# Issuing the on-chip hops of split queries and keys from ScalarE instead of SyncE

## Chip, core and metric

One core of a Trainium2 chip runs the whole kernel as one program. The metric is the device time in microseconds of that core, the median of three runs. Five engines work side by side, each through its own instructions in order: TensorE (PE), VectorE (DVE), ScalarE (ACT), GpSimd (POOL) and SyncE (SP), which issues the DMA transfers. An instruction waits for semaphores that other engines or finished transfers raise.

## What is computed

Two blocks of a network act on 512 tokens of width 1024. The first is a layer of dilated attention, gated linear attention and block attention followed by an MLP with a squared relu; the second has two layers, each with a Fourier mix, attention with rotary tables over the tokens and a context of 256 tokens, a two-way recurrent scan, and a gated MLP. The context goes through the first of the two layers as well. Cut to its frame:

```python
def reference(x, ..., final_norm_w, c_2, ctx_2, ...):
    x = first_block(x, norm1_w, w_in, ..., final_norm_w)
    return second_block(x, c_2, ctx_2, c_ctx_2, w_ada_2, ...)

def hybrid_layer(x, ...):                 # first block
    proj = rmsnorm(x, norm1_w) @ w_in
    y_a, y_b, y_c = dilated_attention(...), gla(...), moba_attention(...)
    x = x + concatenate([y_a, y_b, y_c]) @ w_out
    return x + square(relu(rmsnorm(x, norm2_w) @ w_ff1)) @ w_ff2

def attend(q, k, v):                      # second block's attention
    s = einsum('bkgqd,bksd->bkgqs', q, k) * (HEAD_DIM ** -0.5)
    return einsum('bkgqs,bksd->bkgqd', softmax(s), v)
```

## The kernel before

Activations lie with features on the 128 rows (partitions) and tokens along the free axis. For precise products at the fast rate every operand is split into a high part (rounded to the type R) and a low remainder, and one product becomes three matmuls. Weights come in pieces of 512 KB into one of four `raw` buffers (or two `rawc`, which also take the modulation weights `wada`); ACT casts the high part into a `wu` buffer (three of them) and DVE subtracts to get the low part (`loader`, L689 on).

**Who sets the order.** The order on every engine is made while the program is built, by a list scheduler (`Sched`, L436 on). Each piece of the network is a task that yields operations; each operation carries a cost and a latency from a table in `_op` (L298); the scheduler takes the operation that can start first by its own clocks. So an operation's assigned engine and cost change not only its own place but the order of everything after it. All instructions are emitted in `emit` (L538), and the profile gives nearly all of them line L544; they are told apart by tile names. `slot` is a general buffer of 128x512, `psm`, `psx` and `psd` are PSUM buffers, `pr` and `sm` belong to the softmax.

**The hops.** For attention, one head's 64 rows must stand beside another head's. `stack_q` (L779) splits a pair of query heads: ACT casts the high parts, DVE subtracts, and two transfers copy 64 rows of one buffer to the other 64 rows of the same or another buffer. `stack_k` (L799) does the same for keys, for each of the two heads in turn: one cast, one subtraction, a hop of the high part, a hop of the low part. Of the two hops of a pair, one carries what DVE has just subtracted, the other what ACT cast:

```python
yield V("tensor_tensor", x[:64], q[:64, :n], a[:64], ALU.subtract)
yield V("tensor_tensor", b[64:], q[64:, :n], x[64:], ALU.subtract)
s.free(q)
yield DMA(a[64:].bitcast(F), x[:64].bitcast(F))
yield DMA(b[:64].bitcast(F), x[64:].bitcast(F))
```

`DMA` (L350) makes an SP operation with cost `max(bytes / 360, 460)` ns and latency 2300 ns; a hop costs 460 there. The first block has six head pairs (36 hops, through `att1_pair`); the context has four query pairs and its keys (12 hops of half the size); layer 0 of the second block the same at full size (12), layer 1 as well, with keys of the context beside it (16). That makes 76 hops, 38 pairs of them. SP also issues every weight load, reload and table, all in one order.

Of the kernel before, what the change touches and what calls it, by code (L numbers as in the profile page):

```python
# [9 lines left out]
F = mybir.dt.float32  # L10
# [250 lines left out]
def is_ap(a):  # L261
    return hasattr(a, "tensor") and hasattr(a, "shape")


def free_size(a):
    n = 1
    for d in a.shape[1:]:
        n *= d
    return n


def in_psum(a):
    return a.tensor.name.startswith("ps")


def keys(a):

    nm = a.tensor.name
    if nm[:4] not in ("slot", "psm0", "psm1", "psx0", "psx1"):
        return [nm]  # L280
    lo = hi = a.offset % T
    for st, n in list(a.ap)[1:]:
        if st < 0:
            lo += st * (n - 1)
        else:
            hi += st * (n - 1)
    return [f"{nm}/{h}" for h in range(lo // TC, hi // TC + 1)]


def all_keys(aps):  # L290
    return [k for a in aps for k in keys(a)]
# [6 lines left out]
def _op(eng, fn, args, kw):  # L298
    aps = [x for x in args if is_ap(x)] + [x for k, x in kw.items() if is_ap(x) and k != "accum_out"]
    outs = keys(args[0])  # L300
    if "accum_out" in kw:
        outs += keys(kw["accum_out"])
    if fn == "tensor_tensor_reduce":
        outs += keys(args[-1])
    ins = all_keys(aps[1:])
    n = max(free_size(a) for a in aps)
    table = None
    if eng == "dve":
        per = 1.04
        if fn in ("tensor_copy", "tensor_scalar", "memset") and not any(in_psum(a) for a in aps):  # L310
            per = 0.52
        if fn == "reciprocal":
            per = 6.6
        cost, lat = 62 + n * per + 62 * any(is_ap(a) and free_size(a) == 1 and n > 1 for a in args[2:]), 130
    elif eng == "act":
        extra = sum(1 for k in ("bias", "scale") if is_ap(kw.get(k))) + (fn == "mul" and is_ap(args[2]))
        cost, lat = 90 + n / 1.2 + 90 * extra + (60 if "accum_out" in kw else 0), 160
        for a in args:
            if not is_ap(a) and a in TABLES:
                table = TABLES[a]  # L320
    elif eng == "pool":
        cost, lat = 115 + n * (2.15 if fn == "tensor_tensor" else 3.7), 150
        if fn == "memset":
            cost = 200 + n
    elif eng == "sp":
        b = 4 * free_size(args[0]) * args[0].shape[0]
        cost, lat = max(b / 360.0, 460), 2300
    else:
        raise ValueError(eng)
    op = Op(eng, [(fn, args, kw)], cost, lat, ins, outs, table)  # L330
    if eng == "dve":

        sb = sum(1 for a in aps[1:] if not in_psum(a) and free_size(a) > 1)
        op.port = sb > 1 or (fn in ("tensor_copy", "tensor_scalar") and sb > 0 and not in_psum(args[0]))
    return op


def V(fn, *a, **k):
    return _op("dve", fn, a, k)


def ACT(fn, *a, **k):
    return _op("act", fn, a, k)
# [5 lines left out]

def DMA(*a, **k):  # L350
    return _op("sp", "dma_start", a, k)


def alt(*ops):
# [273 lines left out]
class Kernel:  # L628
# [52 lines left out]
    def load_consts(s, names):  # L681
        shapes = {"masks": ([P, 11, 32], I32), "dmask": ([P, 32], F)}
        for n in names:
            shape, dt = shapes.get(n, ([P, P], F))
            s.c[n] = s.const.tile(shape, dt, name="c_" + n)
            yield DMA(s.c[n], s.A["c_" + n])


    def loader(s, seq, futs, prio=0, raw="raw", hold=None, after={}):  # L689
# [5 lines left out]
        def load():  # L695
            for i, ap in enumerate(seq):
                if i == 1 and hold is not None:
                    yield hold[1]
                for f in after.get(i, ()):
                    yield f  # L700
                r = yield Alloc(raw)
                if i == 0 and hold is not None:
                    r2 = yield Alloc(raw)
                    yield DMA(r[:, :T], ap[:, :T])
                    raws[0].set((r, r2, late))
                    yield hold[0]
                    yield DMA(r2[:, :T], ap[:, T:])
                    late.set()
                else:
                    yield DMA(r, ap)  # L710
                    raws[i].set(r)
# [67 lines left out]
    def stack_q(s, q, n, turn=False):  # L779

        if n == T:
            a, b, x = yield Alloc("slot", R, 3)
        else:
            ab, x = yield Alloc("slot", R, 2)
            a, b = ab[:, :n], ab[:, n:]
            x = x[:, :n]
        if turn:
            q = yield from s.turned(q, n)
        yield ACT("copy", a[:64], q[:64, :n])
        yield ACT("copy", x[64:], q[64:, :n])  # L790
        yield V("tensor_tensor", x[:64], q[:64, :n], a[:64], ALU.subtract)
        yield V("tensor_tensor", b[64:], q[64:, :n], x[64:], ALU.subtract)
        s.free(q)
        yield DMA(a[64:].bitcast(F), x[:64].bitcast(F))
        yield DMA(b[:64].bitcast(F), x[64:].bitcast(F))
        s.free(x)
        return a, b

    def stack_k(s, kf, n, fut, turn=False):  # L799

        k = yield kf
        if n == T:
            t = yield Alloc("slot", R, 4)
        else:
            x, y = yield Alloc("slot", R, 2)
            t = [x[:, :n], x[:, n:], y[:, :n], y[:, n:]]
        if turn:
            k = yield from s.turned(k, n)
        for h in range(2):
            hi, lo = t[2 * h], t[2 * h + 1]  # L810
            own, other = (slice(0, 64), slice(64, P)) if h == 0 else (slice(64, P), slice(0, 64))
            yield ACT("copy", hi[own], k[own, :n])
            yield V("tensor_tensor", lo[own], k[own, :n], hi[own], ALU.subtract)
            yield DMA(hi[other].bitcast(F), hi[own].bitcast(F))
            yield DMA(lo[other].bitcast(F), lo[own].bitcast(F))
        s.free(k)
        fut.set(((t[0], t[1]), (t[2], t[3])))

# [1955 lines left out]
```

## Time and profile before

| | |
|---|---|
| median of three runs | 2242.0 us (2240.91, 2242.0, 2247.69) |
| the profiled execution | 2240.01 us, span of its instructions 2238.2 us |
| PE busy | 2210.3 us (99%) |
| DVE busy | 1560.7 us (70%) |
| ACT busy | 916.4 us (41%) |
| POOL busy | 112.7 us (5%) |
| DMA | 272.69 MB, mean 122 GB/s |
| granted TensorE clock | 0.999 |

A busy PE is a PE with a matmul in its pipeline; gaps shorter than a matmul's way through it don't show as idle. "Idle before" and its arrow name what an engine waited for; the chain of waits is followed back from the last instruction, at each step to what released it.

### The profile page before, as it was taken

How to read it: one execution, taken by the hardware profiler on the slowest of the kernel's cores; microseconds unless marked ns; L12 is line 12 of the kernel's file. 1: busy time of each engine (PE TensorE's matmuls, PEld its weight loads, DVE VectorE, ACT ScalarE, POOL GpSimd, SP SyncE). 2: the span in 40 equal slices, each digit the busy share in tenths (PEclk: the TensorE clock that was granted, in tenths of full speed). 3: DMA queues.
4: the chain of work that ended last, by engine and by line, in shares of the span. 5: the costliest groups of instructions: out<-in, count | busy, mean ns of one | idle time of the engine just before them, and what ended most of it. 6: DMA issues, size and time to landing. Idle time of an engine off the chain costs nothing.

```text
span 2238.2 us, 42398 instructions
## 1 busy us (share of the span) xinstructions
PE 2210.3 (99%) x17071; PEld 1924.0 (86%) x17071; DVE 1560.7 (70%) x3754; ACT 916.4 (41%) x1679; POOL 112.7 (5%) x118
## 2 busy tenths in 40 slices
PE   9999999999999999999999999999999999999998
PEld 7887988788888879899888888889979899888887
DVE  6888976888888898798765443557787876444446
ACT  5465644452224455764212112124545754222224
POOL 0100002000000030000000000000040000000000
PEclk9999999999999999999999999999999999999999
DMA  5446443334444621343333212433321223222223
GB/s 197 139 146 189 176 149 125 137 128 146 146 155 166 216 78 48 104 143 138 144 126 128 95 66 78 136 136 119 113 66 58 77 86 123 94 95 102 96 94 113
DMA packets 92116, 272.69 MB, mean 122 GB/s; under 512 B 10944, under 2 KB 20952, under 8 KB 91920
## 3 DMA queue, kind: packets, MB, share of 16 engines
q1 hardware_dynamic: 91920, 269.99, 35.8%
q8 instruction: 134, 2.20, 0.4%
q14 instruction: 62, 0.51, 0.1%
HBM read 253.66 MB, written 7.38 MB: 117 GB/s over the span
## 4 chain that ended last, share of the span: by engine, by line
PE 91%; DVE 4%; DMA 2%; ACT 2%; issue 1%; SPq 0%; DVEq 0%; ACTq 0%
PE psm L544 69%; PE psx L544 18%; PE psd L544 4%; DVE slot L544 3%; DMA rawc<-wada 1%; DVE wu L544 1%; ACT wu L544 1%; ACT slot L544 1%; DMA slot<-ctx 0%; SPq L544 0%; DMA slot<-x 0%; DMA slot<-slot 0%; DMA rawc<-w2in 0%; ACT pr L544 0%; DVE sm L544 0%
## 5 line engine op out<-in xcount | busy, mean ns | idle before, releaser
L544 PE MATMUL psm<-slot,wu 128*128 128x512 f32 (+1 forms) x8406 | 1542.8, 341 | 6.6 <-DVE slot L544 5.0
L544 PEld LDWEIGHTS psm<-slot,wu 128*128 128x128 f32 x8406 | 1305.6, 190 | 188.1 <-DVE slot L544 8.1
L544 ACT CAST wu<-raw 128x1024 fp32r<-128x1024 f32 (+1 forms) x325 | 340.5, 1048 | 860.0 <-PE psm L544 479.1
L544 DVE TENSOR_TENSOR wu<-raw,wu 128x1024 fp32r<-128x1024 f32 (+1 forms) x325 | 402.3, 1238 | 180.8 <-ACT wu L544 175.5
L544 DVE CUSTOM_DVE_ANT_0 slot<-rawc,slot 128x256 f32<-128x256 f32 x640 | 271.4, 424 | 100.7 <-DMA rawc<-wada 90.5
L544 DVE TENSOR_TENSOR slot<-slot,slot 128x256 f32<-128x256 f32 (+5 forms) x362 | 197.0, 554 | 15.2 <-ACT slot L544 12.5
L544 PE MATMUL psm<-wu,slot 128*128 128x256 f32 x1296 | 181.5, 289 | 0.0
L544 DVE SCALAR_TENSOR_TENSOR slot<-psm,mods,slot 128x256 f32<-128x256 f32 (+1 forms) x190 | 108.5, 572 | 104.4 <-PE psm L544 103.2
L544 DVE TENSOR_TENSOR slot<-slot,psm 128x512 f32<-128x512 f32 (+1 forms) x202 | 118.6, 594 | 76.4 <-PE psm L544 71.5
L544 PEld LDWEIGHTS psm<-wu,slot 128*128 128x128 f32 x1296 | 162.7, 191 | 4.0 <-issue 1.2
L544 PE MATMUL psx<-slot,wu 128*128 128x512 f32 (+1 forms) x858 | 164.1, 346 | 0.1
L544 PEld LDWEIGHTS psx<-slot,wu 128*128 128x128 f32 x858 | 137.1, 190 | 19.2 <-DVE wu L544 0.3
L544 PE MATMUL psd<-slot,slot 64*32 64x32 f32 (+6 forms) x3616 | 124.5, 216 | 6.0 <-issue 2.5
L544 PEld LDWEIGHTS psd<-slot,slot 64*32 64x32 f32 (+4 forms) x3616 | 93.5, 116 | 35.7 <-issue 15.8
L544 PE MATMUL psx<-slot,slot 128*64 128x128 f32 (+5 forms) x1554 | 121.3, 281 | 0.9 <-ACT slot L544 0.7
L544 POOL TENSOR_TENSOR slot<-slot,slot 128x256 f32<-128x256 f32 (+1 forms) x72 | 72.6, 1016 | 951.9 <-DVE slot L544 820.1
L544 ACT CAST slot<-slot 128x512 fp32r<-128x512 f32 (+3 forms) x142 | 79.7, 561 | 77.0 <-DVE slot L544 73.9
L544 PEld LDWEIGHTS psx<-slot,slot 128*64 128x64 f32 (+3 forms) x1554 | 91.1, 139 | 23.3 <-issue 10.9
L544 ACT COPY slot<-psx 128x256 f32<-128x256 f32 (+5 forms) x191 | 78.2, 421 | 61.5 <-PE psx L544 53.0
L544 ACT ACTIVATE slot<-slot 128x256 f32<-128x256 f32 (+1 forms) x150 | 65.3, 456 | 33.3 <-DVE slot L544 28.5
L544 ACT ACTIVATE pr<-psd,sm 128x768 f32<-128x768 f32 (+1 forms) x80 | 65.1, 816 | 19.8 <-DVE sm L544 19.1
L544 DVE SCALAR_TENSOR_TENSOR slot<-slot,mods,slot 128x256 fp32r<-128x256 f32 (+2 forms) x152 | 69.0, 492 | 4.6 <-ACT slot L544 4.5
(100 smaller groups left out, 1334.4 us busy)
## 6 DMA issues: line engine op xcount, KB each, us to landing
rawc<-wada SPq DMA_DIRECT2D x96, 512.0 KB, 4.5
raw<-w2gu SPq DMA_DIRECT2D x88, 512.0 KB, 3.3
raw<-w1ff SPq DMA_DIRECT2D x64, 512.0 KB, 3.3
raw<-w2da SPq DMA_DIRECT2D x56, 512.0 KB, 3.2
raw<-w2in SPq DMA_DIRECT2D x36, 512.0 KB, 3.4
raw<-w2out SPq DMA_DIRECT2D x24, 512.0 KB, 3.7
raw<-w1in SPq DMA_DIRECT2D x23, 512.0 KB, 4.0
rawc<-w2in SPq DMA_DIRECT2D x18, 512.0 KB, 3.3
```

The source lines that it names most:

```text
L544: r = getattr(eng, fn)(*a, **k)
```

## The change

The four `DMA` calls in `stack_q` and `stack_k` become calls of a new function `HOP`. It makes the same transfer, assigns it to ACT instead of SP, and gives it cost 100 instead of 460; the latency stays 2300.

```diff
+def HOP(*a):
+
+    op = _op("sp", "dma_start", a, {})
+    op.eng, op.cost, op.lat = "act", 100, 2300
+    return op
...
-        yield DMA(a[64:].bitcast(F), x[:64].bitcast(F))
-        yield DMA(b[:64].bitcast(F), x[64:].bitcast(F))
+        yield HOP(a[64:].bitcast(F), x[:64].bitcast(F))
+        yield HOP(b[:64].bitcast(F), x[64:].bitcast(F))
...
-            yield DMA(hi[other].bitcast(F), hi[own].bitcast(F))
-            yield DMA(lo[other].bitcast(F), lo[own].bitcast(F))
+            yield HOP(hi[other].bitcast(F), hi[own].bitcast(F))
+            yield HOP(lo[other].bitcast(F), lo[own].bitcast(F))
```

Line numbers after `DMA` grow by 7. The counts of matmuls and of table loads stay the same; ACT gains 76 DMA instructions, SP has 599 where it had 675.

SP in the first block, at the first head pair's hops, with the semaphores that each row waits for (`slot_125` to `slot_141` are the pair's split queries and keys, `raw` and `rawc` weight loads). Before:

```order
L544 DMA raw_128_706<-w1in 128x1024 [waits DMAHW5_49,DVE_49]
L544 DMA slot_125_697<-slot_127_699 64x512 [waits DMAHW6_49,DVE_49]
L544 DMA slot_126_698<-slot_127_699 64x512 [waits DMAHW7_49,Activation_49]
L544 DMA rawc_137_849<-wada 128x1024 [waits DMAHW0_49]
L544 DMA raw_142_866<-w1in 128x1024 [waits DMAHW1_49,DVE_49]
L544 DMA slot_138_853<-slot_138_853 64x512 [waits DMAHW2_49,Activation_49]
L544 DMA slot_139_854<-slot_139_854 64x512 [waits DMAHW3_49,DVE_49]
```

and now:

```order
L551 DMA raw_128_706<-w1in 128x1024 [waits DMAHW5_49,DVE_49]
L551 DMA rawc_137_849<-wada 128x1024 [waits DMAHW7_49]
L551 DMA raw_142_866<-w1in 128x1024 [waits DMAHW1_49,DVE_49]
L551 DMA rawc_164_1018<-wada 128x1024 [waits DMAHW4_49,DMAHW2_49]
L551 DMA slot_98_419<-cl 128x256 [waits DMAHW7_49,DVE_49]
```

The loads follow each other without the hops between them. Each transfer waits for one of eight completion semaphores, DMAHW0 to DMAHW7, taken in turn; the numbers that are missing here belong to the hops, which are now on ACT but still take their turn among the eight.

ACT at the same place, now (before, the four DMA rows are absent and the rest stands in this order):

```order
L551 CAST slot_138_853<-slot_136_814 64x512 [waits DVE_49]
L551 ACTIVATE slot_82_299<-psm_135_813,slot_77_269 128x256 [waits PE_49]
L551 DMA slot_138_853<-slot_138_853 64x512 [waits DMAHW3_49,Activation_49]
L551 DMA slot_139_854<-slot_139_854 64x512 [waits DMAHW4_49,DVE_49]
L551 CAST slot_140_855<-slot_136_814 64x512
L551 DMA slot_140_855<-slot_140_855 64x512 [waits DMAHW5_49,Activation_49]
L551 DMA slot_141_856<-slot_141_856 64x512 [waits DMAHW6_49,DVE_49]
L551 ACTIVATE slot_91_346<-psm_144_889,slot_77_269 128x256 [waits PE_49]
```

The last row, which empties a PSUM buffer of the dense products, now stands behind a hop that waits for DVE.

ACT in layer 0 of the second block, at its keys (`psx_1694` and `psx_1697` hold the turned keys, the COPY rows feed the recurrent scan). Before:

```order
L544 CAST slot_1690_8571<-psx_1694_8575 64x512 [waits PE_49]
L544 COPY slot_1700_8585<-slot_1640_8221 128x256 [waits DMAHW2_49]
L544 COPY slot_1709_8646<-slot_1641_8222 128x256
L544 CAST slot_1692_8573<-psx_1694_8575 64x512 [waits DVE_49]
L544 COPY slot_1709_8646<-slot_1640_8221 128x256 [waits Pool_49]
```

and now:

```order
L551 CAST slot_1693_8556<-psx_1697_8560 64x512 [waits PE_49]
L551 COPY slot_1698_8561<-slot_1638_8200 128x256 [waits DMAHW6_49]
L551 DMA slot_1693_8556<-slot_1693_8556 64x512 [waits DMAHW4_49,Activation_49]
L551 DMA slot_1694_8557<-slot_1694_8557 64x512 [waits DMAHW5_49,DVE_49]
L551 CAST slot_1695_8558<-psx_1697_8560 64x512
L551 COPY slot_1707_8638<-slot_1639_8201 128x256
L551 DMA slot_1695_8558<-slot_1695_8558 64x512 [waits DMAHW6_49,Activation_49]
L551 DMA slot_1696_8559<-slot_1696_8559 64x512 [waits DMAHW7_49,DVE_49]
```

The hops stand between the two casts, and one copy has moved behind the first pair of hops.

## Rows read from the trace of the kernel before

**Rows 1.** The page: span, and busy time by engine with share and instructions.
```profile
span 2238.2 us, 42398 instructions
PE 2210.3 (99%) x17071; PEld 1924.0 (86%) x17071; DVE 1560.7 (70%) x3754; ACT 916.4 (41%) x1679; POOL 112.7 (5%) x118
```

**Rows 2.** Busy time by stretch: the four stretches that hold the hops.
```profile
core 0: us, PE busy (x) PEld busy (x) DVE busy (x) ACT busy (x) POOL busy (x), PEclk, DMA share, GB/s
50.00:216.00 166.00, 164.10 (x1658) 135.58 (x1657) 135.88 (x461) 85.24 (x195) 12.14 (x20) 1.00 0.50 148
364.00:496.00 132.00, 131.20 (x1232) 107.32 (x1231) 116.21 (x321) 63.21 (x136) 22.12 (x23) 1.00 0.38 129
784.00:962.00 178.00, 175.14 (x2337) 150.33 (x2337) 154.29 (x365) 112.56 (x254) 26.90 (x25) 1.00 0.23 74
1612.00:1815.00 203.00, 197.52 (x2547) 172.63 (x2547) 160.07 (x358) 115.07 (x257) 37.49 (x33) 1.00 0.19 60
```

**Rows 3.** Waits of PE over the whole span: waited for, us, times, longest.
```profile
PE psx L544 <- DVE slot L544: 4.9, 7, 1.8
...
PE psx L544 <- ACT slot L544: 1.7, 3, 1.0
...
PE psm L544 <- DVE wu L544: 1.1, 2, 0.7
PE psd L544 <- DMA slot<-slot: 0.3, 1, 0.3
```

**Rows 4.** Tile slot on SP: the hops' issue, ns min/median/max, first and last start.
```profile
L544 SPq DMA_DIRECT2D slot<-slot x76: 461/468/1276, 54.3 to 1762.8; - x76
```

**Rows 5.** Timeline of DVE and of SP, 849 to 854 us (layer 0's queries).
```profile
849.35 0.68 DVE L544 TENSOR_TENSOR slot<-psx,slot 64x512 fp32r<-64x512 f32 x1 [1.84 <-ACT slot L544]
...
850.10 1.11 SPq L544 DMA_DIRECT2D slot<-slot  x2
852.64 0.33 SPq L544 DMA_DIRECT2D raw<-w2outk  x1
853.38 1.10 SPq L544 DMA_DIRECT2D slot<-slot  x2
```

**Rows 6.** Timeline of ACT at the same place.
```profile
848.13 1.19 ACT L544 CAST slot<-psx 64x512 fp32r<-64x512 f32 x2 [0.93 <-PE psx L544]
849.94 1.05 ACT L544 CAST wu<-raw 128x1024 fp32r<-128x1024 f32 x1 [0.62 <-PE psx L544]
```

**Rows 7.** The chain of waits by line, each stretch of rows 2 by itself, in order.
```profile
by line: PE psm L544 41.9%; PE psx L544 15.5%; DMA rawc<-wada 13.0%; PE psd L544 9.3%; DVE slot L544 6.0%; issue 5.8%; DMA slot<-slot 3.0%; DVE wu L544 2.4%; SPq L544 1.9%; ACT wu L544 1.9%; ACT slot L544 1.4%; DVE part L544 0.2%; DVEq L544
...
by line: PE psm L544 67.2%; PE psx L544 23.1%; PE psd L544 6.4%; DVE wu L544 1.4%; ACT wu L544 0.8%; DVE slot L544 0.5%; ACT slot L544 0.5%; issue 0.2%; DVEq L544 0.0%
...
by line: PE psx L544 34.3%; PE psm L544 22.9%; DVE slot L544 14.5%; PE psd L544 14.1%; issue 2.8%; ACT slot L544 2.5%; ACT pr L544 2.4%; DVE wu L544 2.0%; DVE sm L544 1.8%; ACT wu L544 1.1%; ACT sm L544 0.4%; ACT at L544 0.4%; DVE at L544 0
...
by line: PE psx L544 39.1%; PE psm L544 32.9%; PE psd L544 15.9%; DVE slot L544 5.4%; issue 1.9%; ACT wu L544 1.6%; DVE wu L544 1.4%; ACT sm L544 0.6%; ACT slot L544 0.6%; DVE sm L544 0.5%; DVE fin L544 0.1%; DVEq L544 0.0%; ACTq L544 0.0%
```

**Rows 8.** The chain in order of time, 50 to 216 us: start, us, what.
```profile
55.51 4.93 DMA rawc<-wada
...
65.11 4.96 DMA slot<-slot
...
113.85 1.28 SPq L544
115.82 5.17 DMA rawc<-wada
```

**Rows 9.** Timeline of SP, 52 to 57 us and 113 to 117 us.
```profile
54.30 1.16 SPq L544 DMA_DIRECT2D slot<-slot  x2
55.51 0.59 SPq L544 DMA_DIRECT2D rawc<-wada  x1
...
113.85 1.92 SPq L544 DMA_DIRECT2D slot<-slot  x2
115.82 0.58 SPq L544 DMA_DIRECT2D rawc<-wada  x1
```

**Rows 10.** DMA issues from 62.5 to 65.2 us, then from 907 to 908.3 us: median to landing.
```profile
raw<-w1in SPq DMA_DIRECT2D x1, 512.0 KB
slot<-slot SPq DMA_DIRECT2D x4, 128.0 KB, 5.2
...
slot<-slot SPq DMA_DIRECT2D x2, 128.0 KB, 2.3
```

**Rows 11.** Waits of SP's queue over the whole span: us, times, longest.
```profile
SPq L544 <- DVE wu L544: 1266.3, 250, 28.2
```

## The prediction

> **What bounds the kernel now.** I read the page first. PE is busy for 2210.3 of 2238.2 us [rows 1], so all the idle time that PE shows is 28 us; whatever the change does for PE, it can win only out of that and out of waits too short to show. The reader should then look at where the hops run: four stretches hold all 76 of them, and in these PE is busy for 164.10 of 166, 131.20 of 132, 175.14 of 178 and 197.52 of 203 us [rows 2]. That is 1.90 + 0.80 + 2.86 + 5.48 = 11.0 us of idle time in 679 us. DVE is the second busiest there (154.29 of 178 us in layer 0), and ACT stands at 85.24 of 166, 63.21 of 132, 112.56 of 178 and 115.07 of 203 us [rows 2], together 376.1 us, about 55%.
>
> Next, does anybody wait for a hop? PE's waits for one come to 0.3 us, once; its waits for split weights, whose loads share SP's order with the hops, come to 1.1 us [rows 3]. Last, does SP hold the hops back? At layer 0's queries DVE's subtraction ends at 849.35 + 0.68 = 850.03 and SP issues the hop at 850.10 [rows 5]: it goes out as soon as its data is there. So the queue that the change relieves is not what the hops wait for, in this row; and their lateness reaches PE hardly anywhere.
>
> **The change part by part.** The sum is made against the profiled execution, 2240.0 us, which is 2.0 us under the median of 2242.0.
>
> *SP is relieved.* 76 issues leave SP, 468 ns each by the median [rows 4], and a pair takes 1.11 us with its gap [rows 5]: 38 x 1.11 = 42 us. SP only issues, so this counts where a load behind a hop is late for someone. In the first block it is: the chain runs through loads of modulation weights at 55.51 and 115.82 us and through SP itself at 113.85 [rows 8], and these loads stand right behind hops that began at 54.30 and 113.85 [rows 9]. Without the hops they could go out up to 1.2 and 2.0 us sooner, 3.2 us in all. But PE was idle for only 1.9 us in that whole stretch [rows 2]. The bounds are 0 and -3.2; I take -1, nearer to what PE's idle time leaves.
>
> *The hops land sooner.* Four hops right behind a 512 KB load took 5.2 us to land, two with nothing ahead 2.3 us [rows 10]. With a place of their own in the DMA engines the first kind could save up to 2.9 us each. One such landing is on the chain, 4.96 us at 65.11 [rows 8], so at most 4.96 - 2.3 = 2.7 us; what PE showed as a wait for hops is 0.3 us [rows 3]. I take -0.3, since the other landings have other work of PE in front of them.
> Here two statements of the Trainium skill pull apart, both in "DMA: Bandwidth & Descriptors". Its section "Issuing engines are not separate DMA queues" says that transfers started by several engines run on the same 16 DMA engines, interleaved, and that spreading them saves only the issuing engine's time. By that rule alone this term is 0. The section "Queues, rings and completion order" says that SP and ACT own a queue row each and that every DMA engine takes turns between rows packet by packet; by that a hop would pass a load and the term could reach -2.7. No row of the kernel before shows a transfer issued by ACT, so the trace decides neither; my value lies between them.
>
> *ACT issues.* No row shows what an issue costs on ACT. The nearest is the same instruction on SP, 1.11 us a pair [rows 5], so 42 us of ACT's time for all pairs (the scheduler reckons 0.2 us a pair). Besides, ACT now stands still at the one hop of each pair that carries DVE's result: ACT's second cast ended at 848.13 + 1.19 = 849.32 [rows 6] and the subtraction at 850.03, so 0.7 us a pair, 27 us for 38. The bounds are 0 (ACT idles for 45% of these stretches) and 42 + 27 = 69 us (every bit on the path). What part of ACT's time lies on the path can be read off the chain: ACT's lines are 3.3%, 1.3%, 6.8% and 2.8% of it in the four stretches [rows 7], which is 5.5 + 1.7 + 12.1 + 5.7 = 25.0 us of the 376.1 us that ACT was busy, 6.6%. The wait for DVE the scheduler knows and fills with other work where it can; the issue time it doesn't, so I charge that: 42 x 6.6% = +2.8 us. ACT's instructions right behind a hop are the ones to watch: an evacuation of a dense PSUM buffer in the first block, a copy for the recurrent scan in layer 0, exponentials in the queries' part.
>
> *The order is made anew.* A hop that costs 100 instead of 460 on another engine moves the start of everything behind it, and the rows of all engines are reshuffled in the four stretches. The matmuls are the same ones, and the stretches before and after are dense MLP work whose order hardly feels it. A new order can win at most what PE idles there, 11.0 us; it can lose as much just as well. I see no reason for a sign and take 0, with +-11 as bounds.
>
> Sum: -1 - 0.3 + 2.8 + 0 = +1.5, hence 2241.5 us for a profiled execution and with the 2.0 us between that and the median **2243.5 us**. That is no change: a measurement here can tell about 0.3%, 6.7 us.
>
> **The rivals.**
> *ACT becomes the wait (slower).* Place: the attention of layers 0 and 1, where 14 of the 38 pairs stand and where PE's own work is short products that wait for exponentials and evacuations on ACT. Price: 14 x (1.11 + 0.7) = 25 us if all of it lands on PE, about half of it, 13 us, if ACT's other work covers the rest: 2255 us, with 2267 as its end. For it: ACT's share of the chain is largest in layer 0, and the 11 us of the four stretches show that PE has little slack that could absorb it. Against it: ACT is idle for 65 of 178 us there, and PE's largest wait for ACT in the whole span is 1.7 us in three times [rows 3]. It decides from the point where ACT comes later at a pair, by its 1.8 us, than the scheduler has other matmuls in place for PE. It gets 0.20.
>
> *SP's freedom and earlier hops count in full (faster).* All terms that point down reach their ends, or the new order closes the gaps: PE's 11.0 us of idle time in the stretches goes, 2242 - 11 = 2231 us. For it: the chain in the first block does run through SP and through loads behind hops, 13.0% of that stretch by loads of modulation weights and 3.0% by a hop [rows 7]. Against it: PE idles for 1.9 us there, and the three other stretches have no such load in their chains to speak of. It gets 0.20.
>
> *The hops aren't free of SP.* The order shows that hops and loads still take turns at eight completion semaphores, so a hop on ACT waits for the transfer eight places before it, often a load that SP issues. SP stands up to 28.2 us for a buffer that DVE has yet to free [rows 11]. If a hop met such a load, ACT and all behind it would stand with it: one such stop of 28 us, half covered, gives 2242 + 14 = 2256 us. Against it: 675 transfers in 2238 us are one in 3.3 us, so eight places back is some 27 us ago on average, about as long as the longest of these stops. It gets 0.05. In the milder form, that the wait is there but always already over, the change is simply what the sum says.
>
> **How the numbers follow.** No change within 0.3% gets 0.55, from the sum; faster by more 0.20; slower by more 0.20 + 0.05 = 0.25. The likeliest time is the sum's, 2243.5. The range goes from 2231, where all of PE's idle time in the four stretches is gone, to 2257, just over the half price of the first rival and the single stop of the third; the full price of 25 us, or a gain out of waits that PE doesn't show, is the part left out.
>
> **What would show it.** Right: ACT's row of DMA issues is there with some 0.47 us each, ACT's busy time of compute is unchanged near 916 us, PE's idle time in the four stretches stays near 11 us, and PE's waits for hops stay under 1 us. The landing of hops behind loads tells the second term: near 2.3 us if they pass the load, near 5 if not. The forecast is wrong to the slow side if PE's waits for ACT, or DVE's waits for ACT, grow by several us in layers 0 and 1 just behind hops; wrong to the fast side if PE's idle time in the stretches drops to a few us, or if the same matmuls take less time between the same milestones with no idle shown. If the time moves and neither hop, ACT nor SP stands in the new waits, then it was the order.

## The result, and the profile after

The changed kernel takes 2257.24 us (median of 4 runs, 2256.53 to 2262.89); the kernel before, on the same chip, 2241.45 us. The ratio is 1.0076, 95% interval 1.0064 to 1.0088: **slower by 0.76%**, where no change was forecast. (The ratio is made from all the runs and is not the quotient of the two medians; these lie 15.8 us apart, 0.70%.) The profiled execution took 2257.28 us with a span of 2255.5 us, 17.3 us over the span of before.

The page of the changed kernel: span, busy time by engine, and two DMA queues (packets, MB, share).

```profile
span 2255.5 us, 42357 instructions
...
PE 2216.6 (98%) x17071; PEld 1927.8 (85%) x17071; DVE 1551.7 (69%) x3744; ACT 922.1 (41%) x1690; POOL 113.8 (5%) x117
...
q1 hardware_dynamic: 85840, 261.07, 33.9%
q10 hardware_dynamic: 6080, 8.92, 1.6%
```

Against [rows 1] PE has the same matmuls, idles for 2255.5 - 2216.6 = 38.9 us instead of 27.9, and is busy for 6.3 us longer: 11.0 + 6.3 = 17.3 us. The hops are on a queue of their own, q10. What stands against each other is PE's idle time and PE's pace, so I looked for both by stretch. Busy time in the four stretches that hold the same work as [rows 2] (the first is 9 us longer now, the others begin later):

```profile
core 0: us, PE busy (x) PEld busy (x) DVE busy (x) ACT busy (x) POOL busy (x), PEclk, DMA share, GB/s
50.00:225.00 175.00, 166.53 (x1661) 137.82 (x1660) 135.68 (x467) 85.80 (x200) 12.07 (x18) 0.99 0.49 145
372.00:504.00 132.00, 129.90 (x1238) 106.13 (x1237) 109.73 (x293) 66.28 (x146) 22.06 (x20) 1.00 0.37 123
795.00:975.00 180.00, 174.09 (x2331) 150.34 (x2329) 161.16 (x399) 112.30 (x251) 31.31 (x31) 1.00 0.26 83
1629.00:1832.00 203.00, 198.05 (x2545) 172.08 (x2543) 156.98 (x354) 115.83 (x256) 38.35 (x34) 1.00 0.20 62
```

PE idles here for 8.47 + 2.10 + 5.91 + 4.95 = 21.4 us, where it was 11.0. The first block gained 6.6 us of it, layer 0 gained 3.1, the context 1.3, layer 1 nothing. What ends these waits, over the whole span (waited for, us, times, longest):

```profile
PE psm L551 <- DVE slot L551: 5.2, 13, 1.4
PE psd L551 <- DMA slot<-slot: 5.2, 9, 2.1
PE psd L551 <- DVE slot L551: 4.6, 6, 1.5
PE psx L551 <- DVE slot L551: 3.5, 5, 1.8
PE psm L551 <- ACT slot L551: 2.9, 2, 1.7
...
PE psx L551 <- ACT slot L551: 1.5, 3, 1.0
PE psm L551 <- DVE wu L551: 1.3, 1, 1.3
PE psd L551 <- ACT wu L551: 1.2, 1, 1.2
...
PE psd L551 <- ACT slot L551: 1.0, 1, 1.0
```

The first row is no news, since the kernel before has it with 5.0 us. A hop was waited for once, for 0.3 us [rows 3]; now nine times, for 5.2 us. Waits for ACT grew by as much, from 1.7 us to 2.9 + 1.5 + 1.2 + 1.0 = 6.6 us. The chain of the first block (50 to 216 us) says the same: hops hold 16.0% of it, where it was 3.0% [rows 7], and the loads of modulation weights fell from 13.0% to 2.7%.

```profile
by line: PE psm L551 45.1%; DMA slot<-slot 16.0%; PE psx L551 11.7%; PE psd L551 11.2%; DVE slot L551 6.6%; DMA rawc<-wada 2.7%; issue 2.4%; ACT slot L551 1.4%; DVE wu L551 1.3%; ACTq L551 0.6%; ACT wu L551 0.6%; SPq L551 0.3%; DVE sm L551 
```

The longest single wait, in PE's timeline of the changed kernel (start, us, what, and in brackets the idle time before): the first scores of a head pair wait for a hop, and PE stands for 2.12 us.

```profile
120.47 2.20 PE L551 MATMUL psm<-slot,wu 128*128 128x512 f32 x9
122.51 0.42 PE L551 MATMUL psd<-slot,slot 128*128 128x128 f32 x2
125.04 0.30 PE L551 MATMUL psd<-slot,slot 128*128 128x128 f32 x1 [2.12 <-DMA slot<-slot]
125.61 0.84 PE L551 MATMUL psd<-slot,slot 128*128 128x128 f32 x5 [0.27 <-DMA slot<-slot]
126.29 1.44 PE L551 MATMUL psm<-slot,wu 128*128 128x512 f32 x3
```

The last row shows where busy time went: three matmuls of 512 columns take 1.44 us, while nine had taken 2.20. The busy time by stretch, with the granted clock (PEclk) behind the five engines, around this place and two more:

```profile
10.30:13.70 3.40, 3.15 (x8) 2.11 (x8) 3.40 (x6) 3.40 (x7) 0.00 (x0) 0.50 1.01 378
122.60:126.30 3.70, 1.32 (x10) 1.09 (x9) 1.08 (x6) 0.02 (x1) 0.00 (x0) 1.00 0.89 258
126.30:129.70 3.40, 3.40 (x12) 2.94 (x11) 2.77 (x14) 1.84 (x8) 0.40 (x1) 0.50 0.52 143
702.50:706.60 4.10, 2.17 (x9) 1.28 (x8) 3.96 (x12) 1.16 (x2) 0.00 (x0) 1.00 0.30 100
706.60:710.00 3.40, 3.40 (x9) 2.65 (x9) 1.18 (x5) 1.25 (x2) 0.00 (x0) 0.50 0.50 190
```

Twice PE waited and was then granted 0.50, which is 1.2 GHz, while it was fully busy. The stretch at 10.30 us lies ahead of all hops, and there too PE had waited. It waited 1.19 us for ACT, whose cast had waited for a weight load (PE's row first, then ACT's):

```profile
9.95 0.54 PE L551 MATMUL psm<-slot,wu 128*128 128x512 f32 x1 [1.19 <-ACT slot L551]
8.51 0.62 ACT L551 CAST wu<-raw 128x512 fp32r<-128x512 f32 x1 [1.32 <-DMA raw<-w1in]
```

That load goes out at 2.60 us in both kernels, yet the kernel before has no wait for ACT here and a granted clock of 1.00. Of the runs below, e1, with the order of before, waits 0.29 us here and e2, with the changed order, 0.33 us, both at full clock. So some 3 us at the start (1.2 of idle time, up to 1.7 of half clock) go with a load that landed late in this execution, and not with the change. Three stretches of 3.4 us at half pace cost up to 3 x 1.7 = 5.1 us, most of the 6.3 us of added busy time.

So most of the time went to waits of PE in the first block and layer 0 and to half clock behind them. Two explanations remain: ACT's issuing, or the new order.

### The profile page after: what moved, and what is told of

Its sections match the earlier page's. It is cut to its first block, busy times and chain, and to the rows that moved or that the text cites. A ratio compares the mean times of both kernels' runs of the same rounds, so it can differ in the third digit from the quotient of the medians.

```text
span 2255.5 us, 42357 instructions
## 1 busy us (share of the span) xinstructions
PE 2216.6 (98%) x17071; PEld 1927.8 (85%) x17071; DVE 1551.7 (69%) x3744; ACT 922.1 (41%) x1690; POOL 113.8 (5%) x117
## 4 chain that ended last, share of the span: by engine, by line
PE 91%; DVE 4%; DMA 2%; issue 1%; ACT 1%; POOL 0%; SPq 0%; ACTq 0%; DVEq 0%; POOLq 0%
PE psm L551 69%; PE psx L551 18%; PE psd L551 4%; DVE slot L551 3%; DMA slot<-slot 1%; DVE wu L551 1%; ACT slot L551 1%; DMA rawc<-wada 0%; ACT wu L551 0%; DMA slot<-x 0%; POOL slot L551 0%; DVE sm L551 0%; ACT at L551 0%; SPq L551 0%; ACTq L551 0%
## 5 line engine op out<-in xcount | busy, mean ns | idle before, releaser
L551 DVE TENSOR_TENSOR slot<-slot,slot 128x256 f32<-128x256 f32 (+4 forms) x360 | 197.2, 558 | 15.4 <-ACT slot L551 13.0
L551 PE MATMUL psx<-slot,wu 128*128 128x512 f32 (+1 forms) x918 | 170.7, 341 | 0.0
L551 PEld LDWEIGHTS psx<-slot,wu 128*128 128x128 f32 x918 | 143.9, 190 | 18.5
L551 PE MATMUL psx<-slot,slot 128*64 128x128 f32 (+8 forms) x1554 | 121.0, 281 | 0.7 <-ACT slot L551 0.5
L551 ACT COPY slot<-psx 128x512 f32<-128x512 f32 (+4 forms) x199 | 81.6, 423 | 72.0 <-PE psx L551 63.8
L551 PEld LDWEIGHTS psx<-slot,slot 128*64 128x64 f32 (+4 forms) x1554 | 90.8, 139 | 23.5 <-issue 9.0
L551 DVE TENSOR_REDUCE sm<-psd 128x1 f32<-128x768 f32 (+1 forms) x80 | 66.4, 844 | 7.8 <-PE psd L551 7.1
```

The lines of the kernel that those rows point to most:

```text
L551: r = getattr(eng, fn)(*a, **k)
```

## The experiments

In the expectations, theory A says that issuing on ACT costs the time. Against it stands the order, in two forms: C, the scheduler promises each hop too soon (100 + 2300 ns in the change, 460 + 2300 before) and so puts the scores too early; D, orders scatter whatever the reason, and D2, which the later runs take up, that the order of before is an unusually good one, so that nearly any new one costs. "The scheduler's own sum" is the end of PE's work by the scheduler's clocks, worked out while the program is built; it is no measured time.

All results, each beside the kernel before on the same chip; "idle" is span less PE's busy time, and "hops" PE's waits for hops between 40 and 290 us, both from one execution of each kernel, the profiled one. Executions of one kernel differ: those of the kernel before, 21 beside u1, took 2239.37 to 2250.48 us. The profiled one of e1 took 2252.01 us, 5.4 us over its median, so its last two columns are on the high side. The ratios are made from all the runs, as above:

| run | median us | before us | ratio [95%] | idle | hops |
|---|---|---|---|---|---|
| before | | | | 27.9 | 0.3 |
| the change | 2257.24 | 2241.45 | 1.0076 [1.0064, 1.0088] | 38.9 | 5.0 |
| e1_sp_order_act_issue | 2246.58 | 2245.08 | 1.0010 [1.0000, 1.0020] | 33.8 | 4.6 |
| e2_act_order_sp_issue | 2266.56 | 2245.08 | 1.0095 [1.0081, 1.0110] | 42.5 | 3.9 |
| e3_act_cost550 | 2252.05 | 2245.08 | 1.0028 [1.0017, 1.0039] | 35.0 | 2.3 |
| n1_sp_cost100 | 2247.86 | 2245.08 | 1.0011 [1.0002, 1.0020] | 32.1 | 1.5 |
| h1_first_block_only | 2264.42 | 2243.43 | 1.0090 [1.0071, 1.0108] | 42.4 | 3.3 |
| h2_second_block_only | 2252.15 | 2243.43 | 1.0036 [1.0023, 1.0049] | 36.0 | 0.9 |
| a1lat_act_cost100_lat2660 | 2253.36 | 2243.43 | 1.0043 [1.0027, 1.0059] | 34.8 | 3.1 |
| n2_sp_lat2200 | 2247.82 | 2243.43 | 1.0014 [1.0003, 1.0025] | 33.6 | 0.3 |
| u1_sync62 | 2252.68 | 2243.51 | 1.0042 [1.0028, 1.0055] | 36.5 | 1.2 |
| u2_dve63 | 2254.99 | 2243.51 | 1.0057 [1.0044, 1.0070] | 37.3 | 0.6 |
| act460_lat2600 | 2244.83 | 2243.51 | 1.0013 [1.0004, 1.0022] | 30.6 | 1.8 |
| n3_sp_cost600 | 2247.95 | 2243.51 | 1.0015 [1.0005, 1.0024] | 31.4 | 0.8 |
| act_sync58 | 2245.41 | 2246.29 | 0.9994 [0.9985, 1.0003] | 30.9 | 1.6 |
| act_sync54 | 2255.48 | 2246.29 | 1.0047 [1.0033, 1.0060] | 38.5 | 1.9 |
| n4_sp_cost50 | 2254.30 | 2246.29 | 1.0037 [1.0023, 1.0050] | 34.2 | 3.0 |

### Order and issuing engine apart

A new field tells `emit` which engine issues, apart from the engine that the scheduler reckons with. e1 keeps the order of before on all compute engines and issues the hops from ACT; e2 keeps the order of the change and issues them from SP.

```diff
+        s.on = eng
...
-        eng = s.eng[e]
+        eng = s.eng[op.on]
...
-    op.eng, op.cost, op.lat = "act", 100, 2300
+    op.on = "act"
```

(in e2 the line with `op.eng` stays, and `op.on = "sp"` follows it).

> The order on PE, DVE, POOL and of ACT's own work is that of the kernel before, row for row; only the 76 hops leave SP and are issued by ACT at their place in the order. Theory A (ACT's issuing is the cost: 42 us of issue time and the waits for DVE hold up what ACT does next): most of the loss is here too, 2250 to 2257 us. Theory B (the cost lies in the new order that the scheduler makes when it takes a hop for 100 ns on ACT): 2239 to 2245 us, as before.

> The order on PE, DVE, POOL and of ACT's own work is that of the changed kernel, row for row; the hops are issued by SP as before. Theory A: the loss goes, 2239 to 2246 us. Theory B: the loss stays, 2252 to 2260 us, or grows, since SP holds the hops back behind its loads in an order that was made for a free queue.

With ACT's issuing alone the kernel is 1.5 us over before (0.1%, interval 0 to 0.2%): 1.6 us above theory B's range, and well under theory A's. With the new order alone it is 0.95% slower, at least as much as the change, and beyond the 2260 us of theory B. So **the loss goes with the order**. The hops do hold PE up in e1's profiled execution, 4.6 us in the table, and in e2's, 3.9 us. So waits for hops come with either half of the change, and alone they don't make the loss; their landing in e1 is below.

### What the scheduler is told

```diff
-    op.eng, op.cost, op.lat = "act", 100, 2300
+    op.eng, op.cost, op.lat = "act", 550, 2300
```

is e3; n1 has `op.cost = 100` on SP, n2 `op.lat = 2200` on SP, and a1lat `"act", 100, 2660`, which promises a landing at the 2760 ns of before.

> Hops on ACT as in the change, but the scheduler is told 550 ns for each, about what an issue with its gap takes in the traces, instead of 100. Theory A, that ACT's unreckoned time hurts: better than the change, 2243 to 2250 us, since the order now allows for it. Theory B in its plain form, that any new order here costs at random: anywhere between 2240 and 2260 us, with no relation to the cost.

> Hops on SP as before; only the scheduler's cost of a hop goes from 460 to 100 ns, which reorders 567 lines of PE's difference instead of 1499. Theory A: 2239 to 2245 us. Theory B: part of the loss, 2244 to 2254 us, because the hops are planned 360 ns sooner than they come.

> Hops on ACT, cost 100 as in the change, but latency 2660 instead of 2300, so that the plan has a hop land when it had it land on SP (460 + 2300). Theory C (the plan promises the hops 360 ns too soon, and PE then stands before the first scores): most of the loss in the first block goes, 2244 to 2250 us. Theory D (a new order is a draw, and the change drew a bad one): no relation, 2240 to 2260 us.

> A control for Theory D: hops on SP as before, only their planned latency 100 ns shorter, 2200. Nothing that the hardware does for a hop changes. Theory C: 2244 to 2248 us. Theory D: the order (588 lines of PE's difference) moves the time by itself, up or down by up to 10 us.

A later promise goes with less loss on ACT: 2400 ns gives 1.0076, 2760 gives 1.0043, 2850 gives 1.0028, and PE's waits for hops fall from 5.0 to 3.1 to 2.3 us. On SP a shorter promise costs 0.1%, with little wait for hops. So C may tell part of it; each of these kernels also has an order of its own. e3 missed A's range (2243 to 2250 us) and a1lat missed C's (2244 to 2250 us), both to the slow side.

### Half of the hops at a time

```diff
-        yield HOP(a[64:].bitcast(F), x[:64].bitcast(F))
+        yield (DMA if turn else HOP)(a[64:].bitcast(F), x[:64].bitcast(F))
```

and so in the other three lines: `turn` is there in the second block only. h1 has ACT's hops in the first block, h2, with the two names exchanged, in the second.

> ACT issues the hops of the first block alone (36), the context's and the two layers' stay with SP. In the profile of the change 8 of its 17 us were lost before 300 us and the rest after 690 us. If each part's order does its own harm, this has the first half: +6 to +10 us, and layer 0 runs as before. If what goes wrong in a part comes from how the scheduler's order falls out by chance, the later part may come out anyhow: +0 to +20 us.

> ACT issues the hops of the context and the two layers alone (40); the first block's order is that of the kernel before. If each part does its own harm: +5 to +10 us, lost between 690 and 1060 us, with the same gaps of PE as in the change (1.6 us before the first products of the recurrent scan in layer 0). If ACT's wait at the keys' hops of layer 0 is what makes these gaps, they stand beside DMA issues on ACT.

The parts do not add up: h1 alone loses 0.90%, 21.0 us, more than the whole change and more than either of its expectations; h2 loses 0.36%, 8.7 us, as expected. In layer 0 h1's hops are on SP as before, yet PE waits longer there. From 690 to 1060 us the kernel before waits 3.1 us for VectorE, and this is its largest row:

```profile
PE psm L544 <- DVE slot L544: 2.0, 2, 1.4
```

In h1 it waits 10.9 us for VectorE, and for no hop:

```profile
PE psd L551 <- DVE slot L551: 4.5, 5, 2.0
PE psm L551 <- DVE slot L551: 3.5, 5, 1.4
PE psx L551 <- DVE slot L551: 2.9, 3, 2.4
PE psd L551 <- ACT pr L551: 1.4, 2, 1.0
```

So an order disturbed in the first block goes on to cost in layer 0, where nothing of the hops was changed. C has no place for that, D has. Nor does A: the wait of 1.7 us ahead of layer 0, which the change shows at 705.61 us and h2 at 699.96, stands where ACT issues no hop. The last before it goes out in the context, and layer 0's first at 799.52 us.

### New orders that have nothing to do with hops

The kernel before, its hops untouched, with one number of the scheduler moved by 2 ns or by 1 ns:

```diff
-    SYNC = 60
+    SYNC = 62
```

```diff
-        cost, lat = 62 + n * per + 62 * any(...), 130
+        cost, lat = 63 + n * per + 62 * any(...), 130
```

> The kernel before, hops on SP and planned as they were; only the scheduler's allowance for a hand-over between engines is 62 ns in place of 60, so the order is made anew for a reason that has nothing to do with hops. Theory D2 (the order of before is an unusually short one, and any new order costs, whatever the reason): slower by 5 to 13 us, 2248 to 2257, with layer 0 as a main place, and no more than 2 us of PE waits for hops. Theory C (the loss comes of hops that are promised too soon): no change, within 3 us of before. By the scheduler's own sum this order ends 5.9 us later than that of before, and the order of the change 4.2 us later.

> The kernel before, hops on SP and planned as they were; only the fixed cost of a VectorE instruction is taken as 63 ns in place of 62. Theory D2: slower by 9 to 22 us, 2252 to 2266 (by the scheduler's own sum this order ends 10.3 us later than that of before, the longest of the orders tried). Theory C: no change, within 3 us of before.

Slower by 0.42% and 0.57%, as D2 expected and C did not, with waits for hops of 1.2 and 0.6 us in the table (2.0 and 0.6 over the whole span). In u1 the largest waits are for DVE. PE's waits over the whole span of u1:

```profile
PE psx L544 <- DVE slot L544: 10.1, 8, 3.9
```

and the longest of them in PE's timeline of u1, in layer 0, where a product with the buffer `at` stands for DVE's result:

```profile
934.22 0.70 PE L544 MATMUL psx<-at,slot 128*64 128x128 f32 x4 [3.87 <-DVE slot L544]
```

**A new order can cost this much with every hop left alone.** These two were taken for their long sums, 5.9 and 10.3 us over before, so they don't tell what a new order costs on average.

### Hops on ACT in a better order

act460_lat2600 is the change with `"act", 460, 2600`; n3 has hops on SP with `op.cost = 600`.

> The change, with a hop reckoned at 460 ns on ScalarE and 2600 ns to landing, which is nearer to what the trace shows; by the scheduler's own sum this is the shortest of the orders with hops on ScalarE (2.2 us over before, the change 4.2). Theory D2: about half of the change's loss, 3 to 9 us over before, 2247 to 2253. Theory C: likewise less than the change, since the landing is promised 0.66 us later, and PE's waits for hops fall from 5.2 to under 3 us. Theory A (ScalarE's issuing is what costs): unchanged at 2257, since the 76 issues still stand on ScalarE.

> Hops on SP as before, but reckoned at 600 ns in place of 460, so that each is promised 0.14 us later than before. Theory D2: slower by 5 to 14 us, 2248 to 2258 (by the scheduler's own sum 6.4 us over before). Theory C: no loss, within 3 us of before or faster. Theory A: no change, ScalarE issues nothing.

With all 76 hops issued by ACT the loss shrinks to 0.13%, which A excludes; D2 expected more, 3 to 9 us. n3 came out at 4.4 us over before, just under D2's 5 to 14 and over C's 3.

act_sync58 and act_sync54 both have

```diff
-    op.eng, op.cost, op.lat = "act", 100, 2300
+    op.eng, op.cost, op.lat = "act", 460, 2800
```

and `SYNC = 58` in the one, `SYNC = 54` in the other. n4 has hops on SP with `op.cost = 50`, which gives the shortest sum.

> Hops on ScalarE, reckoned at 460 ns and 2800 ns to landing, with the scheduler's allowance for a hand-over at 58 ns in place of 60; by the scheduler's own sum the order ends 0.9 us later than that of before, the shortest found with hops on ScalarE. Theory D2 (only the order counts): within 4 us of before, 2241 to 2248, and PE's waits for hops at 2 us or less. Theory A (hops on ScalarE cost of themselves): 2250 or more.

> As act_sync58 with 54 ns in place of 58, so hops, their engine and their promised landing are the same; by the scheduler's own sum the order ends 6.0 us later than that of before. Theory D2: slower than act_sync58 by 3 to 12 us, 2247 to 2257. Theory A or C: equal to act_sync58 within 3 us.

> Hops on SP, reckoned at 50 ns in place of 460; by the scheduler's own sum the order ends 0.6 us sooner than that of before. Theory D2 alone: 2239 to 2246. Theory C (promised too soon, by 0.41 us each): PE waits for hops again in the first block, 2 to 5 us, and 2246 to 2250 in all.

act_sync58 runs as fast as before (0.9994, interval 0.9985 to 1.0003) **with every hop on ACT**; act_sync54, with the same hops and the same promise, loses 0.47%. The first block shows it, 40 to 290 us; act_sync58 first, then act_sync54:

```profile
PE psd L551 <- DMA slot<-slot: 1.6, 2, 1.4
PE psd L551 <- issue: 1.4, 1, 1.4
```

```profile
PE psd L551 <- issue: 6.4, 3, 3.1
PE psx L551 <- DVE slot L551: 2.4, 2, 2.2
PE psd L551 <- DMA slot<-slot: 1.9, 2, 1.6
```

Hops cost about the same in both. The largest difference is 5.0 us of "issue", a wait for which the profile names nothing. Two gaps make up nearly all of act_sync54's: 3.12 and 3.00 us, each ahead of the last 8 of 64 small products, a series that act_sync58 runs in 0.75 us without a gap (at 51.32 us).

```profile
52.76 0.26 PE L551 MATMUL psd<-slot,slot 32*32 32x32 f32 x8 [3.12 <-issue]
```

What PE lacked there is open, so this pair shows that the order decides and not how. act_sync54 also ran at half clock behind the two gaps, as its busy time by stretch shows in the column behind POOL:

```profile
53.20:56.60 3.40, 3.40 (x9) 2.68 (x9) 3.40 (x7) 0.00 (x0) 0.77 (x1) 0.51 0.15 33
73.70:80.50 6.80, 6.80 (x152) 6.22 (x150) 4.32 (x22) 2.45 (x9) 0.64 (x1) 0.50 0.00 2
```

n4 misses what D2 alone said (2239 to 2246) and also goes past C's 2250, with C's waits: the shortest sum does not make the fastest kernel where hops are promised 2350 ns and take longer. No version here beats the kernel before.

## Why the prediction was wrong

**The step that failed is the fourth term**, "The order is made anew": "I see no reason for a sign and take 0, with +-11 as bounds". Fourteen kernels of this study have an order of their own (all but e1 and e2). Thirteen of them are slower than before with intervals clear of 1, one is the same, none is faster; their mean is +0.36%, about 8 us. The six with hops on SP have a mean of +0.29%, the eight with all or half of the hops on ACT +0.41%. (They are no random draw: u1 and u2 were taken for long sums of the scheduler, act460_lat2600, act_sync58 and n4 for short ones.) So the term had a sign, and its middle was some +8 us. The bound was wrong too: "it can lose as much just as well" bounds a loss by the present idle time, but PE was made to wait where it hadn't, and some of the waits had half clock behind them. This order came to some 14 us (15.8 less the 1.5 of e1), and h1's kernel to 21.0 in all.

The loss is made of two things. Of the 17.3 us by which the profiled execution is longer, 11.0 are idle time of PE and up to 5.1 are half clock; some 3 of these us go with the late load at its start, which the change didn't bring. Waits for hops give 4.9 of the 11.0 (5.2 against 0.3), waits for ACT another 4.9 (6.6 against 1.7, with 1.2 of the late load), waits for DVE 1.9 (16.3 against 14.4). Waits for hops fall where the promise is later: on ACT 2400 ns gives 5.0 us (3.3 in h1), 2760 gives 3.1, 2850 gives 2.3, 3060 gives 1.8 and 3260 gives 1.6 and 1.9. The promise is not all of it, for e1 keeps the order made for 2760 ns and shows 4.6. Without a change of hops, u1 shows the other kind: a wait of 3.87 us for DVE's work that isn't ready. Which of the scheduler's decisions makes each of them I have not traced, and the scheduler's own sum tells only in part: n3 with +6.4 us by that sum lost 4.4, n4 with -0.6 lost 8.0.

**The sum of the other terms held, the terms did not all.** They summed to -1 - 0.3 + 2.8 = +1.5; e1, which is just these three, measured 2246.58 - 2245.08 = +1.5, interval 0 to 4.5 us. That the two numbers are equal is luck: the interval is wide, and the second term was wrong, as e1's waits for hops show (4.6 us, where the prediction had under 1). What the first and the third are worth by themselves no run shows. The price of an issue was right (tile `slot` on ACT, ns min/median/max, as [rows 4] on SP):

```profile
L551 ACTq DMA_DIRECT2D slot<-slot x76: 468/469/1059, 55.4 to 1781.3; - x76
```

*The hops land sooner* did not come true in the first block. Median landing of the 36 hops between 40 and 290 us, the kernel before and then e1, where the compute engines have the same order:

```profile
slot<-slot SPq DMA_DIRECT2D x36, 128.0 KB, 4.0
```

```profile
slot<-slot ACTq DMA_DIRECT2D x36, 128.0 KB, 4.9
```

In the changed kernel the median there is 4.0 us, as before. Behind 300 us the kernel before and e1 give:

```profile
slot<-slot SPq DMA_DIRECT2D x24, 128.0 KB, 3.1
```

```profile
slot<-slot ACTq DMA_DIRECT2D x24, 128.0 KB, 2.7
```

So a queue of their own did not take the hops past the loads where these are dense, and gained 0.4 us where PE had not waited for hops. That loads which SP lets out sooner meet the hops in the first block would explain the 4.9; it was not measured. The rule of the Trainium skill, "DMA: Bandwidth & Descriptors", section "Issuing engines are not separate DMA queues", was the nearer one in the first block: only the issuing engine's time is saved, and the 4.0 and 4.9 us show no gain in landing. What the section "Queues, rings and completion order" of the same page says of turns between rows would fit the gain behind 300 us, which was worth nothing to PE.

**The rivals.** "ACT becomes the wait" named 2255 us, near the result, by a mechanism that isn't it: PE's waits for ACT grew (6.6 us against 1.7), but e2 has 4.5 us of them with no hop on ACT, and act_sync58 loses nothing with all hops on ACT. "SP's freedom" came true in the chain, where loads fell from 13.0% to 2.7%, and PE's idle time in that stretch grew all the same. "Not free of SP" left no stop of that kind: the longest issue took 1059 ns, and of the waits that the profile lists for ACT in the changed kernel the longest is 7.5 us.

**What would show it** had its last sentence wanting: hops and ACT do stand in the new waits, and still most of the loss was the order's.

## What to carry to other kernels

Where a list scheduler orders a kernel, a change of one cost is two changes: the instruction moved, and a new order. Measure them apart, by freezing the order and changing only who issues. And compare the new order with a few orders made anew for no reason (here 1 or 2 ns in an unrelated number): the kernel at hand was one of the best of its kind, thirteen of the fourteen redone orders cost 0.1 to 0.9%, and so an edit should be judged at an order of equal quality. Tell a scheduler landings as the trace shows them, not the cost of an idle queue.

## What was not expected of the hardware

A wait of PE can cost more than itself: behind those of 2.1 us in the first block and 1.7 us ahead of layer 0, in the windows above, the granted clock stood at 0.50 for 3.4 us of full work, up to 1.7 us each. The kernel before shows a mean clock of 0.999 with 27.9 us of idle time, the change 0.996 with 38.9, e2 and h1 0.994 with 42.5 and 42.4. The link is loose: h2 idles for 36.0 us at 0.999.

An issue on ACT did not stop ACT's other instructions. In ACT's timeline of the changed kernel hops are issued in the midst of the softmax:

```profile
127.07 0.49 ACT L551 ACTIVATE slot<-slot,sm 128x256 f32<-128x256 f32 x1
127.31 0.47 ACTq L551 DMA_DIRECT2D slot<-slot  x1
127.47 0.19 ACT L551 ACTIVATION_READ_ACCUMULATOR slot<-slot,sm 128x1 f32 x1
127.56 0.49 ACT L551 ACTIVATE slot<-slot,sm 128x256 f32<-128x256 f32 x1
```

The issue from 127.31 to 127.78 lies beside two instructions that run and one that begins. That may be why 76 issues of 0.47 us, 36 us in all, came to 1.5 us with everything else.
